# Attention probabilities enter the product with V undivided; the row sums are applied later, when the product is fetched for the merge

## The chip, the cores and the metric

One core of one Trainium2 chip runs the whole program. The metric is the device time of one execution in microseconds (us). PE is the engine for matrix products (TensorE), PEld its loading of weights, DVE VectorE, ACT ScalarE, POOL GpSimd, SP the engine that issues nearly all DMAs. Every engine works through its own instructions in order; they meet through semaphores.

## The reference, cut to what matters

One layer of an encoder for 1024 prompt tokens and 32 sample tokens. The part that matters here is sparse attention with 8 heads of 64 columns, and the merge behind it:

```
score  = indexer scores, masked block-causally;  idx = top-k keys per query
logits = (q . k_sel) / 8 + t5_bias ;  p = softmax(logits)          # per query row
a      = p . v_sel                                                   # (tokens, 512)
merged = sigmoid(g_A) * (a @ w_pa) + sigmoid(g_R) * (r @ w_pr)
x1     = LN(alpha * x + merged @ w_o);   y = LN(alpha * x1 + SwiGLU(x1))
```

`softmax` divides each row of exponentials by its sum. The division commutes with the product with V: it can be applied to a row of `p`, or to the same row of `a`.

## The kernel before, in words

All 1056 tokens are cut into nine tiles t (eight of 128, one of 32). Products are made in float32 by splitting each operand into a high and a low part (`split`: ACT writes `hi`, DVE or POOL the difference `lo`) and adding three products on PE.

PE's order is not left to the scheduler: a planner (`Weave`) keeps a clock `W.t` and one list of busy times for ACT, DVE and POOL ("a", "v", "p"), and every generator yields the planned time from which it may go on. The main generator issues a product, then every side generator whose time has come issues one. The order of the other engines is made by a scheduler from the program.

Around the change stand three pieces. `g_jobs` (main) makes the two branch gates: 16 blocks b of 24 column products for each of three column chunks j (384, 384, 288 tokens) into two PSUM banks `g`. While attention runs, ACT evicts them (L729); once attention is over (`"rt" in st`), DVE does (L726). `front` makes, for each head h and tile t, the bias plus mask on POOL (L774), the logits on PE (L783, L785), adds and takes the maximum on DVE (L787, with L795 where a row has two pieces, and L796), the exponential on ACT (L797), the reciprocal of the row sum (L799) and the scaled row (L800) on DVE, in place in `P`. `P_at` tells the planner when the row is ready. `back` transposes P on PE (L837, L838), splits it into `ph` and `pl`, multiplies by V (L861, L862; L867 for the sample tile), adds two halves (`av`, L878, L880) and stores the head's 64 columns to DRAM (`at_d`).

When the last head is done, `fetch` loads the retention output (`rT`) and the attention output (`aT`) of chunk 0 and `rT` of chunk 1, and splits them; the last gate chunks cover that. `aT` of chunks 1 and 2 is fetched when the gates are done, into memory that the activations x held until then. `c_jobs` then multiplies: for each block pair g, chunk j and block i, 24 products from `rT`, then 12 from `aT`, then the sigmoids, two products and a sum on DVE (L967, L968, L970), and a store.

Of the kernel before, what the change touches and what calls it, by code (L numbers as in the profile page):

```python
# [10 lines left out]
F32 = mybir.dt.float32  # L11
# [3 lines left out]
ALU = mybir.AluOpType  # L15
# [85 lines left out]
def mm(n, passes=1):  # L101
    return passes * max(256, n) / 2400.0


def body(ctx, tc, nc, a):
    W = Weave()
# [19 lines left out]
    def f32(ap):  # L126
        return ap.bitcast(F32)

    def dma(out, in_):
        nc.sync.dma_start(f32(out) if out.dtype == F32R else out, f32(in_) if in_.dtype == F32R else in_)  # L130
# [10 lines left out]
    ident = const.tile([128, 128], F32, name="ident")  # L141
    mhalf = const.tile([128, 4], F32, name="mhalf")

    def split(hi, lo, src, hi_eng="pool", lo_eng="pool"):
        if hi_eng == "pool":
            nc.gpsimd.tensor_scalar(hi, src, 1.0, 1.0, op0=ALU.mult, op1=ALU.mult)
        elif hi_eng == "act":
            nc.scalar.activation(hi, src, AF.Copy)  # L148
        else:
            nc.vector.tensor_copy(hi, src)  # L150
        e = nc.gpsimd if lo_eng == "pool" else nc.vector
        e.tensor_tensor(lo, src, f32(hi), op=ALU.subtract)  # L152
# [65 lines left out]
    def scratch(n, shape, name, dt=F32):  # L218
        return [dp.tile(shape, dt, name=f"{name}{i}") for i in range(n)]
# [5 lines left out]
    rt_d, at_d = scratch(1, [D, TT], "rtd")[0], scratch(1, [512, TT], "atd")[0]  # L225
    mt_d = [dp.tile([D, n], F32, name=f"mtd{j}") for j, (_, n) in enumerate(CHUNKS)]
    hd_d, x1_d = scratch(FB, [128, 1024], "hd"), scratch(1, [TT, D], "x1d")[0]
    r_d, r32_d = scratch(1, [8, 1152], "rd")[0], scratch(1, [8, 32, 1152], "r32")[0]

    xp = Open("xp")  # L230
# [16 lines left out]
    def mbank():  # L247
        return psum.tile([128, 512], F32, name="m", bufs=6)
# [261 lines left out]
    st = {}  # L510
# [221 lines left out]

    c_units = []

    def fetch(j, tl, dd, kt):
        c0, n = CHUNKS[j]
        hi, lo = tl
        for k in range(0, kt, 4):
            dma(lo[:, k:k + 4], dd[k * 128:(k + 4) * 128, c0:c0 + n].rearrange("(k p) c -> p k c", p=128))
            for z in range(k, k + 4, 2):  # L740
                split(hi[:, z:z + 2], lo[:, z:z + 2], f32(lo[:, z:z + 2]), "act", "dve")

    def to_attention():
        rp.close()
        xsp.close()
        tk.close()
        W.lag["v"] = 0.2
        st["att"] = True
        st["go"] = attention()

    def attention():
        ap = st["ap"] = Open("att", side="right")
# [4 lines left out]
            load_head(1, i)  # L757
        seq = [(h, t) for h in range(8) for t in range(9)]
        P, P_at, back_done, l_free = {}, {}, {}, []
        front_n = [0]  # L760
        NP = 6

        def front():
            for i, (h, t) in enumerate(seq):
                QS, KS, KL, TB, V = heads[h]
                c0, n = SEGS[t]
                Wd, k0, b0 = ((t + 1) * 128, 0, 896 - c0) if t < 8 else (LS, 1024, 896 - PAST)
                if i >= NP:
                    while seq[i - NP] not in back_done:
                        yield 0.0, W.t + 0.3  # L770
                    yield 0.0, back_done[seq[i - NP]]
                pp = ap.tile([128, 1024], F32, name="P", bufs=NP)
                P[h, t] = pp
                nc.gpsimd.tensor_tensor(pp[0:n, :Wd], TB[0:n, b0:b0 + Wd], masks[t][0:n, :], op=ALU.add)  # L774
                tt = W.on("p", 0.1 + Wd / 480, W.t)
                mx = ap.tile([128, 5], F32, name="mx", bufs=NP)
                halves = list(range(0, Wd, 512))
                for q, n0 in enumerate(halves):
                    nn = min(512, Wd - n0)
                    if len(l_free) >= 2:  # L780
                        yield 0.0, max(l_free[-2], tt - 1.0)
                    L = mbank()
                    nc.tensor.matmul(L[0:n, 0:nn], lhsT=QS[:, c0:c0 + n],  # L783
                                     rhs=KS[:, k0 + n0:k0 + n0 + nn], start=True, stop=False)
                    nc.tensor.matmul(L[0:n, 0:nn], lhsT=QS[:, c0:c0 + n],  # L785
                                     rhs=KL[:, k0 + n0:k0 + n0 + nn], start=False, stop=True)
                    nc.vector.tensor_tensor_reduce(out=pp[0:n, n0:n0 + nn], in0=L[0:n, 0:nn], in1=pp[0:n, n0:n0 + nn],  # L787
                                                   scale=1.0, scalar=-3e38, op0=ALU.add, op1=ALU.max,
                                                   accum_out=mx[0:n, q:q + 1])
                    c = 2 * mm(nn)  # L790
                    tt2 = W.on("v", 0.1 + nn / 930, max(tt, W.t + c))
                    l_free.append(tt2)
                    yield c, W.t
                if len(halves) == 2:
                    nc.vector.tensor_tensor(mx[0:n, 0:1], mx[0:n, 0:1], mx[0:n, 1:2], op=ALU.max)  # L795
                nc.vector.tensor_scalar(mx[0:n, 2:3], mx[0:n, 0:1], -1.0, None, op0=ALU.mult)  # L796
                nc.scalar.activation(pp[0:n, :Wd], pp[0:n, :Wd], AF.Exp, bias=mx[0:n, 2:3], scale=1.0,  # L797
                                     accum_out=mx[0:n, 3:4])
                nc.vector.reciprocal(mx[0:n, 4:5], mx[0:n, 3:4])  # L799
                nc.vector.tensor_scalar(pp[0:n, :Wd], pp[0:n, :Wd], mx[0:n, 4:5], None, op0=ALU.mult)  # L800
                tt = W.on("v", 0.2, tt2)
                tt = W.on("a", 0.35 + Wd / 1150, tt)
                P_at[h, t] = W.on("v", 0.2 + Wd / 1900, W.on("v", 0.1, tt))
                if t == 8 and h + 2 < 8:
                    for i in range(5):
                        load_head(h + 2, i)
                yield 0.0, W.t

        def back():
# [4 lines left out]
            while ia < len(items):  # L814
                opts = []
                if it < len(items) and it - ia < 3:
                    h, g, kb = items[it]
# [7 lines left out]
                h, g, kb = items[it if is_t else ia]  # L825
                last = 2 * g + 1 if g < 4 else 8
                c = 0 if kb < last else 128
                if is_t:
# [3 lines left out]
                    pt = mbank()  # L832
# [38 lines left out]
                if kb == last or g == 4:  # L871
                    for t in ((2 * g, last) if g < 4 else (8,)):
                        back_done[h, t] = W.t + cost
                    n, q0 = (256, g * 256) if g < 4 else (32, T)
                    u = ap.tile([64, 256], F32, name="av", bufs=2)
                    w = n if g < 4 else 64
                    nc.scalar.activation(u[:, :w], po[64:128, :w], AF.Copy)
                    nc.vector.tensor_tensor(u[:, :w], po[0:64, :w], u[:, :w], op=ALU.add)  # L878
                    if g == 4:
                        nc.vector.tensor_tensor(u[:, 0:32], u[:, 0:32], u[:, 32:64], op=ALU.add)  # L880
                    o_free = W.on("v", 0.35, W.on("a", 0.28, W.t + cost))
                    dma(at_d[h * 64:(h + 1) * 64, q0:q0 + n], u[:, :n])
                yield cost, W.t
            ap.close()
            st["hA"].close()
# [4 lines left out]
                  for j, (_, n) in enumerate(CHUNKS)]  # L890
            st["aT"] = [[st["rt"].tile([128, 4, n], F32R, name=f"aT{i}_{j}") for i in range(2)]
                        for j, (_, n) in enumerate(CHUNKS[:1])]
            st["rTt"] = rT
            fetch(0, rT[0], rt_d, 8)
            fetch(0, st["aT"][0], at_d, 4)
            fetch(1, rT[1], rt_d, 8)

        return front(), back()

    W.main(g_jobs())  # L900
# [22 lines left out]
    aT = st["aT"]  # L923
    for j, (_, n) in enumerate(CHUNKS):
        if j:
            aT.append([cp.tile([128, 4, n], F32R, name=f"aT{i}_{j}") for i in range(2)])
    fetch(1, aT[1], at_d, 4)
    fetch(2, rT[2], rt_d, 8)
    fetch(2, aT[2], at_d, 4)
    ringC = Open("ringC", bufs=3)  # L930

    def c_jobs():
# [77 lines left out]
    op = Open("wo", side="right")  # L1010
# [459 lines left out]
```

## Time and profile before

| | |
|---|---|
| runs, us | 1911.21, 1913.57, 1917.74; median 1913.57 |
| profiled execution, us | 1910.34, of which 1908.6 from the first to the last instruction |
| PE busy | 1860.3 us (97% of the span), 11361 products |
| DVE, ACT, POOL busy | 1308.2, 714.3, 741.8 us (69%, 37%, 39%) |
| mean granted PE clock | 0.993 of full |
| DMA | 233.12 MB, mean 122 GB/s |

Busy time is a mean over stages with different limits; where a stage can be shortened is read from the waits within it. A PE clock below 1 in a stretch means that products there took longer. Times in the rows below are from the start of the span.

### The profile page before, as it was taken

What the parts mean: (1) busy time and instruction counts of PE and PEld (TensorE: products, weight loads), DVE (VectorE), ACT (ScalarE), POOL (GpSimd) and SP (SyncE); (2) the same over time, 40 slices, a digit from 0 to 9 for tenths busy, and PEclk for the clock granted to TensorE, in tenths of its full rate; (3) what the DMA queues carried; (4) which work ended last, traced back from release to release, by engine and by line L of the source; (5) the groups of instructions that cost most, each with busy time, mean ns of one, the idle gap of its engine ahead of it and who ended that gap; (6) DMA issues with size and microseconds to landing.
All of it is one profiled execution on the core that took longest, in us unless ns stands there. A gap on an engine that the chain in (4) does not pass through costs nothing. (4 is left out here: it accounts for less than half of the span.)

```text
span 1908.6 us, 30961 instructions
## 1 busy us (share of the span) xinstructions
PE 1860.3 (97%) x11361; PEld 1687.5 (88%) x11361; DVE 1308.2 (69%) x2702; ACT 714.3 (37%) x1492; POOL 741.8 (39%) x741
## 2 busy tenths in 40 slices
PE   8999999999999999999999999999999999999998
PEld 7899899877888898899999879999999999877776
DVE  4799898999992877876533368855555555376667
ACT  5543422424333555555422246432333333432212
POOL 5345633455456435342321133143343333462211
PEclk9999999999999999999999999999999999999999
DMA  6245832223334765544644653122222222542212
GB/s 190 89 146 198 272 130 86 64 77 94 84 88 137 185 164 158 139 115 133 205 156 148 192 165 110 62 72 67 79 90 76 68 89 89 197 162 85 91 42 91
DMA packets 154368, 233.12 MB, mean 122 GB/s; under 512 B 18960, under 2 KB 118280, under 8 KB 154216
## 3 DMA queue, kind: packets, MB, share of 16 engines
q1 hardware_dynamic: 148168, 223.57, 37.6%
q10 hardware_dynamic: 6048, 7.57, 1.2%
q8 instruction: 89, 1.46, 0.3%
q14 instruction: 63, 0.52, 0.1%
HBM read 164.79 MB, written 67.48 MB: 122 GB/s over the span
## 5 line engine op out<-in xcount | busy, mean ns | idle before, releaser
L152 POOL TENSOR_TENSOR wlo<-raw,whi 128x1024 fp32r<-128x1024 f32 (+2 forms) x85 | 199.6, 2354 | 353.8 <-ACT whi L148 290.4
L148 ACT ACTIVATE whi<-raw 128x1024 fp32r<-128x1024 f32 (+1 forms) x158 | 137.1, 881 | 204.0 <-PE m L172 34.3
L172 PE MATMUL g<-xh,whi 128*128 128x384 f32 (+1 forms) x600 | 199.1, 332 | 5.7 <-DVE gev L726 5.7
L172 PE MATMUL g<-xh,wlo 128*128 128x384 f32 (+1 forms) x600 | 199.1, 332 | 0.2 <-POOL wlo L152 0.2
L172 PE MATMUL g<-xl,whi 128*128 128x384 f32 (+1 forms) x600 | 198.8, 331 | 0.0
L377 DVE MAX8 m<-sc 128x8 f32<-128x384 f32 (+6 forms) x209 | 182.4, 875 | 4.7
L378 DVE MATCH_REPLACE8 sc<-m,sc 128x384 f32<-128x384 f32 (+6 forms) x209 | 180.0, 861 | 0.2
L774 POOL TENSOR_TENSOR P<-TB,mask 128x128 f32<-128x128 f32 (+8 forms) x72 | 92.6, 1303 | 115.3 <-PE m L837 91.8
L172 PEld LDWEIGHTS g<-xh,whi 128*128 128x128 f32 x600 | 113.9, 190 | 8.8 <-DVE gev L726 6.2
L172 PEld LDWEIGHTS g<-xl,whi 128*128 128x128 f32 x600 | 114.0, 190 | 2.8 <-issue 1.1
L172 PEld LDWEIGHTS g<-xh,wlo 128*128 128x128 f32 x600 | 114.1, 190 | 2.4 <-POOL wlo L152 0.5
L1309 DVE TENSOR_TENSOR yo<-m,yo 128x512 f32<-128x512 f32 x128 | 85.4, 686 | 43.3 <-PE m L172 41.7
L1212 PE MATMUL m<-T,whi 128*128 128x264 f32 x624 | 114.6, 283 | 0.0
L172 PE MATMUL g<-whi,xl 128*128 128x512 f32 x256 | 105.4, 412 | 0.0
L172 PE MATMUL g<-whi,xh 128*128 128x512 f32 x256 | 104.9, 410 | 0.0
L172 PE MATMUL g<-wlo,xh 128*128 128x512 f32 x256 | 104.1, 407 | 0.0
L1212 PEld LDWEIGHTS m<-T,whi 128*128 128x128 f32 x624 | 96.6, 188 | 0.0
L172 PE MATMUL m<-rT,whi 128*128 128x384 f32 (+1 forms) x384 | 90.7, 322 | 0.0
L1192 POOL TENSOR_TENSOR raw<-raw,qs 128x512 f32<-128x512 f32 x20 | 32.0, 1602 | 149.5 <-DVE wlo L152 95.0
L1212 PE MATMUL m<-T,wlo 128*128 128x264 f32 x312 | 88.6, 284 | 0.0
L1212 PE MATMUL m<-x,whi 128*128 128x264 f32 x416 | 78.7, 288 | 4.4 <-DVE u L1220 4.1
L152 DVE TENSOR_TENSOR wlo<-raw,whi 128x512 fp32r<-128x512 f32 (+1 forms) x79 | 68.0, 874 | 18.3 <-ACT whi L148 17.4
(332 smaller groups left out, 5543.2 us busy)
## 6 DMA issues: line engine op xcount, KB each, us to landing
raw<-wT SPq DMA_DIRECT2D x33, 512.0 KB, 3.8
raw<-w_gate SPq DMA_DIRECT2D x22, 512.0 KB, 3.4
raw<-w_up SPq DMA_DIRECT2D x22, 512.0 KB, 3.4
hd<-sg SPq DMA_DIRECT2D x22, 512.0 KB, 3.2
raw<-w_down SPq DMA_DIRECT2D x22, 512.0 KB, 3.5
raw<-hd SPq DMA_DIRECT2D x22, 512.0 KB, 3.5
raw<-wr SPq DMA_DIRECT2D x16, 512.0 KB, 3.7
ml<-mtd SPq DMA_DIRECT2D x16, 512.0 KB, 4.6
```

Source lines behind the costliest of these rows:

```text
L148: nc.scalar.activation(hi, src, AF.Copy)
L152: e.tensor_tensor(lo, src, f32(hi), op=ALU.subtract)
L172: nc.tensor.matmul(out, lhsT=l, rhs=r, start=i == 0, stop=i == m - 1)
L377: nc.vector.max(m8[0:n], v)
L378: nc.vector.match_replace(v, m8[0:n], v, TAKEN)
L774: nc.gpsimd.tensor_tensor(pp[0:n, :Wd], TB[0:n, b0:b0 + Wd], masks[t][0:n, :], op=ALU.add)
L1192: nc.gpsimd.tensor_tensor(a12, a12, self.s2, op=ALU.subtract)
L1212: nc.tensor.matmul(o, lhsT=w[l][:, k, :], rhs=b[r][:, k, s], start=z < 4 and k == 0 and j == 0, stop=k == 3 and j == 2, skip_group_check=True)
L1309: nc.vector.tensor_tensor(y, src, y, op=ALU.add)
```

## The change

The exponential now writes its row sum into a tile `rsum` that holds the nine sums of a head in nine columns (set to 1.0 first, since the sample tile fills 32 rows only). The reciprocal and the scaling of P are gone, and the planner counts the row as ready when ACT is done with it. After the sample tile of a head, PE transposes `rsum` to nine rows of 128, DVE takes their reciprocal out of PSUM, and a DMA stores them to DRAM (`ri_d`). `fetch` of `aT` loads these rows again, each head's row spread over the 64 partitions of its columns (four DMAs for each half of a chunk, into one buffer `ri`), multiplies `aT` by them on DVE into `ri`, and splits from there.

```diff
+    ri_d = scratch(8, [9, 128], "ri")
...
-    def fetch(j, tl, dd, kt):
+    def fetch(j, tl, dd, kt, rows=False):
...
             for z in range(k, k + 4, 2):
-                split(hi[:, z:z + 2], lo[:, z:z + 2], f32(lo[:, z:z + 2]), "act", "dve")
+                src = f32(lo[:, z:z + 2])
+                if rows:
+                    ri = st["rt"].tile([128, 2, 384], F32, name="ri", bufs=1)
+                    for h in range(2 * z, 2 * z + 4):
+                        dma(ri[h % 2 * 64:h % 2 * 64 + 64, h // 2 - z, :].rearrange("p (t c) -> p t c", c=128),
+                            ri_d[h][None, c0 // 128:c0 // 128 + 3, :].to_broadcast([64, 3, 128]))
+                    nc.vector.tensor_tensor(ri[:, :, :n], src, ri[:, :, :n], op=ALU.mult)
+                    src = ri[:, :, :n]
+                split(hi[:, z:z + 2], lo[:, z:z + 2], src, "act", "dve")
...
+        rsum = {}
...
-                mx = ap.tile([128, 5], F32, name="mx", bufs=NP)
+                mx = ap.tile([128, 3], F32, name="mx", bufs=NP)
+                if t == 0:
+                    rsum[h] = ap.tile([128, 9], F32, name="rsum", bufs=2)
+                    nc.vector.memset(rsum[h], 1.0)
...
                 nc.scalar.activation(pp[0:n, :Wd], pp[0:n, :Wd], AF.Exp, bias=mx[0:n, 2:3], scale=1.0,
-                                     accum_out=mx[0:n, 3:4])
-                nc.vector.reciprocal(mx[0:n, 4:5], mx[0:n, 3:4])
-                nc.vector.tensor_scalar(pp[0:n, :Wd], pp[0:n, :Wd], mx[0:n, 4:5], None, op0=ALU.mult)
+                                     accum_out=rsum[h][0:n, t:t + 1])
                 tt = W.on("v", 0.2, tt2)
-                tt = W.on("a", 0.35 + Wd / 1150, tt)
-                P_at[h, t] = W.on("v", 0.2 + Wd / 1900, W.on("v", 0.1, tt))
+                P_at[h, t] = W.on("a", 0.35 + Wd / 1150, tt)
...
                     dma(at_d[h * 64:(h + 1) * 64, q0:q0 + n], u[:, :n])
+                    if g == 4:
+                        pt = mbank()
+                        nc.tensor.transpose(pt[0:9, 0:128], rsum[h], ident)
+                        rr = ap.tile([9, 128], F32, name="rrow", bufs=1)
+                        nc.vector.reciprocal(rr, pt[0:9, 0:128])
+                        dma(ri_d[h], rr)
...
-            fetch(0, st["aT"][0], at_d, 4)
+            fetch(0, st["aT"][0], at_d, 4, True)
...
-    fetch(1, aT[1], at_d, 4)
+    fetch(1, aT[1], at_d, 4, True)
     fetch(2, rT[2], rt_d, 8)
-    fetch(2, aT[2], at_d, 4)
+    fetch(2, aT[2], at_d, 4, True)
```

The change also moves instructions, in three places. Outside attention, the transition behind it and the merge, the order on every engine is as before (two of the memsets stand ahead of attention).

First, PE within a head. The planner fills PE's planned waits in attention with gate products. From the first logits to the last product with V it now places 475 gate products where it placed 843; the other 368 follow behind attention, so that 22 gate chunks are evicted by DVE there instead of 6. Here is the stretch of PE at the start of the fourth head, from the products with V to the transposes of its tiles 4 and 5 (`P`; `m` is a PSUM bank, `g` a gate bank). Before:

```order
L838 MATMUL m<-ident,P 128x128
L861 MATMUL m<-ph,V 128x256
L862 MATMUL m<-pl,V 128x256
L861 MATMUL m<-ph,V 128x256
L862 MATMUL m<-pl,V 128x256
L172 MATMUL g<-xh,wlo 128x384
L172 MATMUL g<-xh,whi 128x384
L172 MATMUL g<-xl,whi 128x384
...
L837 MATMUL m<-ident,P 128x128
L838 MATMUL m<-ident,P 128x128
```

The line of dots stands for four more gate products. And now:

```order
L848 MATMUL m<-ident,P 128x128
L871 MATMUL m<-ph,V 128x256
L872 MATMUL m<-pl,V 128x256
L871 MATMUL m<-ph,V 128x256
L872 MATMUL m<-pl,V 128x256
L847 MATMUL m<-ident,P 128x128
L848 MATMUL m<-ident,P 128x128
```

The seven gate products ahead of the transposes are gone. From the logits of tile 3 of this head to these transposes PE has 16 gate products where it had 27.

Second, DVE at the same place: from the logits of tile 3 to those of tile 5. Before:

```order
L796 TENSOR_SCALAR mx<-mx 128x1
L878 TENSOR_TENSOR av<-m,av 64x64
L880 TENSOR_TENSOR av<-av 64x32
L787 ISA P,mx<-m,P 128x512
...
L787 ISA P,mx<-m,P 128x128
L787 ISA mx 128x1
L799 RECIPROCAL mx<-mx 128x1
L795 TENSOR_TENSOR mx<-mx 128x1
L800 TENSOR_SCALAR P<-P,mx 128x512
L796 TENSOR_SCALAR mx<-mx 128x1
```

And now (L800 is here the former L787, L808 the former L795, L809 the former L796):

```order
L897 RECIPROCAL rrow<-m 9x128
L789 MEMSET rsum 128x9
L809 TENSOR_SCALAR mx<-mx 128x1
L888 TENSOR_TENSOR av<-m,av 64x64
L800 ISA P,mx<-m,P 128x512
...
L800 ISA P,mx<-m,P 128x128
L800 ISA mx 128x1
L890 TENSOR_TENSOR av<-av 64x32
L808 TENSOR_TENSOR mx<-mx 128x1
L809 TENSOR_SCALAR mx<-mx 128x1
```

The scaling of tile 3 and its reciprocal no longer stand ahead of the maximum of tile 4 (the last row of both pieces); a reciprocal of nine rows and a memset stand ahead of the maximum of tile 3 (the first row of the piece before, the third of the piece now).

Third, the merge: what SP issues once its chunks begin. `aT` of chunks 1 and 2 and the first gate rows stand where they stood; the rows `ri` come in groups of four between them (numbers are those of the DRAM tiles, one for each head):

```order
L130 DMA raw<-w_pa 128x1024
L130 DMA raw<-w_pr 128x1024
L130 DMA ri<-ri_140 64x384
L130 DMA ri<-ri_141 64x384
L130 DMA ri<-ri_142 64x384
L130 DMA ri<-ri_143 64x384
L130 DMA mtd_110<-mm 128x384
L130 DMA ga<-ga_91 128x384
L130 DMA gr<-gr_99 128x384
L130 DMA raw<-w_pr 128x1024
L130 DMA mtd_110<-mm 128x384
L130 DMA ga<-ga_92 128x384
```

Before, the first two of these rows were followed at once by the store of `mm`. Two more such groups follow, for the two halves of chunk 2; the group for the first half of chunk 1 is issued while the gates still run.

## Rows read from the trace of the kernel before

**Rows 1.** Stretches: length; busy PE, PEld, DVE, ACT, POOL; PE clock, DMA share, GB/s.

```profile
613.80:886.50 272.70, 261.75 (x1762) 249.22 (x1761) 210.52 (x701) 152.90 (x406) 119.82 (x82) 0.99 0.54 145
886.50:919.00 32.50, 26.83 (x156) 26.19 (x155) 18.06 (x23) 13.33 (x19) 4.75 (x2) 0.95 0.65 226
919.00:949.00 30.00, 30.00 (x184) 30.00 (x183) 12.57 (x19) 14.29 (x22) 10.56 (x5) 1.00 0.65 220
```

**Rows 2.** Timeline of PE in attention: products that PE waited for (idle before).

```profile
627.36 0.58 PE L862 MATMUL m<-pl,V 128*128 128x256 f32 x1 [2.31 <-DVE pl L152]
664.66 0.33 PE L838 MATMUL m<-ident,P 128*128 128x128 f32 x1 [1.66 <-DVE mx L796]
...
696.68 0.33 PE L838 MATMUL m<-ident,P 128*128 128x128 f32 x1 [0.28 <-DVE mx L796]
...
731.24 0.33 PE L838 MATMUL m<-ident,P 128*128 128x128 f32 x1 [2.47 <-DVE mx L796]
...
798.28 0.47 PE L838 MATMUL m<-ident,P 128*128 128x128 f32 x1 [2.54 <-DVE P L800]
```

**Rows 3.** Timelines of DVE, ACT and POOL ahead of the wait that ends at 731.24.

```profile
725.57 1.45 DVE L880 TENSOR_TENSOR av<-av 64x32 f32<-64x32 f32 x1
...
727.87 0.97 DVE L795 TENSOR_TENSOR mx<-mx 128x1 f32<-128x1 f32 x1
728.76 2.42 DVE L800 TENSOR_SCALAR P<-P,mx 128x512 f32<-128x512 f32 x1
...
725.97 0.18 ACT L797 ACTIVATION_READ_ACCUMULATOR P<-P,mx 128x1 f32 x1
...
725.31 5.59 POOL L774 TENSOR_TENSOR P<-TB,mask 128x768 f32<-128x768 f32 x3
```

**Rows 4.** Timeline of DVE one head earlier: the scaling of tiles 3 and 5.

```profile
696.15 0.47 DVE L800 TENSOR_SCALAR P<-P,mx 128x512 f32<-128x512 f32 x1
...
701.22 0.62 DVE L800 TENSOR_SCALAR P<-P,mx 128x768 f32<-128x768 f32 x1
```

**Rows 5.** Lines L800, L799 and L795 (min/median/max ns, first and last start).

```profile
L800 DVE TENSOR_SCALAR P<-P,mx x72: 286/549/2640, 620.5 to 877.4; 128x128 f32<-128x128 f32 x8, 128x256 f32<-128x256 f32 x8, 128x384 f32<-128x384 f32 x8, 128x512 f32<-128x512 f32 x8
...
L799 DVE RECIPROCAL mx<-mx x72: 140/153/167, 619.9 to 877.2; 128x1 f32<-128x1 f32 x64, 32x1 f32<-32x1 f32 x8
...
L795 DVE TENSOR_TENSOR mx<-mx x40: 136/159/1860, 627.7 to 875.8; 128x1 f32<-128x1 f32 x32, 32x1 f32<-32x1 f32 x8
```

**Rows 6.** Timeline of PE: two gate products, one behind the other.

```profile
732.02 0.34 PE L172 MATMUL g<-xh,wlo 128*128 128x384 f32 x1
732.20 0.34 PE L172 MATMUL g<-xh,whi 128*128 128x384 f32 x1
```

**Rows 7.** The stretch behind the wait that ends at 798.28 (columns as in rows 1).

```profile
798.30:810.00 11.70, 11.70 (x65) 11.35 (x66) 9.36 (x33) 6.76 (x16) 2.03 (x2) 0.88 0.44 130
```

**Rows 8.** Transition: the longest wait of PE, and the splits of rT on DVE (grouped by line).

```profile
909.83 0.45 PE L172 MATMUL g<-xh,whi 128*128 128x384 f32 x1 [4.72 <-DVE gev L726]
...
L152 DVE TENSOR_TENSOR rT<-rT,rT 128x768 fp32r<-128x768 f32 (+1 forms) x12 | 11.6, 1017 | 6.9 <-ACT rT L148 6.9
```

**Rows 9.** DMAs: issue of a row block on SP, and landing (KB each, median us).

```profile
L130 SPq DMA_DIRECT2D atd<-av x40: 445/452/467, 631.5 to 890.8; - x40
...
atd<-av SPq DMA_DIRECT2D x32, 64.0 KB, 1.9
...
ga<-ga SPq DMA_DIRECT2D x4, 192.0 KB, 4.0
```

**Rows 10.** Timelines of ACT, DVE and POOL in the merge.

```profile
924.95 2.85 ACT L148 ACTIVATE aT<-aT 128x768 fp32r<-128x768 f32 x4 [3.86 <-DMA aT<-atd]
...
932.25 2.48 DVE L970 TENSOR_TENSOR mm<-ga,gr 128x384 f32<-128x384 f32 x1
...
938.41 0.56 DVE L970 TENSOR_TENSOR mm<-ga,gr 128x384 f32<-128x384 f32 x1
...
931.90 5.09 POOL L152 TENSOR_TENSOR wlo<-raw,whi 128x1024 fp32r<-128x1024 f32 x2 [6.92 <-ACT whi L148]
```

## The prediction

> **What bounds the kernel now.** The page first: PE is busy for 97% of the span, so work taken off DVE is worth only what PE waits for it. How much that is, the stretches around the change say [rows 1]. In the first, attention (613.8 to 886.5), PE is busy for 261.75 of 272.70 us: 10.95 us idle. In the transition (886.5 to 919.0) it is 5.67 idle. In the first chunks of the merge it is none. The reader is to see that DVE is at 77% in attention and still not the bound: its busy time counts only at the moments when PE stands still.
>
> Next, where those moments are [rows 2]. One wait of 2.31 us belongs to the start. The others come once in each head, at the transposes of tiles 2 and 3, and are of two sizes: three of 1.66, 2.47 and 2.54 us, and four of 0.27 to 0.30, of which one stands in the rows. Two more, of 0.16 and 0.60, lie elsewhere. Sum: 10.9.
>
> Then the large ones taken apart [rows 3]. ACT had finished the exponential at 726.15. The row was usable only at 731.18, since DVE came to its scaling late and the scaling itself took 2.42 us, where the same shape one head earlier took 0.47 [rows 4]. POOL was working through three additions from 725.31 to 730.90; the all-SBUF steps of DVE (0.97 us for one column, then 2.42) end about when POOL's instructions do. Over the run the scaling lasts from 0.29 to 2.64 us, its median 0.55 [rows 5].
>
> This is what a rule of the Trainium skill states (SBUF — State Buffer, "Who interferes with whom"): VectorE and GpSimd share one pair of SBUF ports, and an instruction of VectorE that uses both ports, or reads two SBUF operands, waits for the whole of GpSimd's instruction. The trace agrees here: 2.42 against 0.47 us.
>
> **The change part by part.** *Scaling and reciprocal removed.* In a head without the block, from the logits of tile 3 to the finished rows of tiles 4 and 5, DVE loses three reciprocals of 0.153 [rows 5], one scaling of 0.47, one of 0.62, and one of the width between, which I take at 0.54 as an estimate from these two [rows 4]: 2.1 us. It gains a reciprocal of nine rows and a memset, which the trace does not show; each lies between nothing and the 0.47 of the scaling, and nearest to the one-column reciprocal, so 0.15 to 0.2 each. The chain gets about 1.75 us shorter. PE's cover over the same stretch loses 11 gate products, which follow one another at 0.18 us [rows 6]: 2.0 us shorter, less the transpose added. The planner has taken as much cover away as the chain gave back. So heads that waited 0.3 us will wait about that again, 0.3 to 0.6. What really goes is the blocked scaling, in three heads. The one-column maximum L795 (up to 1.86 us [rows 5]) and L880 stay and can still be blocked, so I take 0.5 us for each of seven heads: 3.5, plus the 2.31 of the start and the 0.76 elsewhere, 6.6 in place of 10.95. **Term: -4.4.** Bounds: all head waits gone, -7.8; each head waiting for an L795 blocked at its longest, 7 x 1.86 + 3.1 = 16.1, +5.1.
>
> *Clock.* After the 2.54 us wait the granted clock is 0.88 over 11.7 us [rows 7], 1.4 us lost; most of that goes with the wait. **Term: -1.2** (0 to -1.4).
>
> *Transposes of the sums.* Eight, on PE, and their results are waited for by no product. Each has a third of the columns of a gate product that takes 0.18; the row of a transpose that was waited for shows 0.33 for its whole length [rows 2]. I take 0.11 each: **+0.9** (0.5 to 2.6).
>
> *Gate products moved.* 368 of them leave attention, where they took the same 0.18 us, and form a run without anything between. They cost the same there; evictions move from ACT to DVE, which then has little else. **0.** If PE had to wait for an eviction it would be in the transition, next.
>
> *Transition.* Today PE waits 4.72 us there, for an eviction that stands on DVE behind splits of `rT` and `aT` [rows 8]. With the change the fourth gate eviction again stands behind eight DVE instructions of that kind: four of `rT`, one multiplication, one of `aT`, two of `rT` (before: six of `rT`, two of `aT`). The rows `ri` put 0.39 MB into a transfer queue that is busy, 1.7 us at the 226 GB/s of the stretch [rows 1]. The multiplication makes a chain of three (DVE, ACT, DVE), but `rT` arrives no earlier than that ends. **0**, between -1.5 and +2.5.
>
> *Merge.* This is where the change adds a wait. Counted from the first merge product (919.0, the third stretch), PE comes to the second half of `aT` of chunk 1 at 17.9 us (two chunks of 6.3, then 24 + 6 products at 0.18), and to the second half of chunk 2 at 29.2. `aT` lands at 5.95 [rows 10], and the split follows at once today, so PE has 10 us to spare. Now the single buffer `ri` makes the four halves serial: multiply (1.0, as a split of `rT` [rows 8]), ACT 0.8 [rows 10], DVE 0.9, then four issues of 0.45 us [rows 9], then the landing of 98 KB. For the landing the trace gives 1.9 us for 64 KB in attention and 4.0 for 192 KB in this very stretch [rows 9]; I take 2.7. First half split at 8.8, new rows at 13.3. There two of POOL's subtractions run, from 12.9 to 18.0 [rows 10], and an all-SBUF sum of DVE took 2.48 us next to them against 0.56 without [rows 10]. So the multiplication ends near 16.4, ACT at 17.2, DVE near 19: PE is 1 to 1.5 us late. Two more rounds of 2.1 to 2.7 for the work and 4.5 for the rows bring the last half to about 33 against the 29.2 of the plan. All waits of the merge together are that lateness, between 2 and 4: **+3.0**. Bounds: nothing, if POOL is not in the way and the rows land in 1.9 us (the last half is then ready at 27.3); 7, if they land in 4.0 and each multiplication is blocked.
>
> By the port rule above the multiplication, which reads two SBUF operands, must wait for POOL's instruction. By it the merge costs about 3; if it did not hold for this operation, close to nothing. This changes only how near the lower bound is.
>
> **Sum:** -4.4 - 1.2 + 0.9 + 0 + 0 + 3.0 = -1.7 us, against the profiled execution of 1910.34: 1908.6. The median of the runs stands 3.2 us above that execution, so 1911.9; I say **1912**. That is no change that a measurement of this kernel can tell (about 0.3%, 5.7 us, on either side of 1913.6: below 1907.8 or above 1919.3).
>
> **The rivals.**
> *Full gain.* All head waits vanish (-7.8), and the rows come in time (merge 0): -7.8 - 1.2 + 0.9 = -8.1, so 1905.5. For it: in the unblocked heads the exponential ends well before PE needs the row. Against: the cover of 11 gate products has gone too.
> *The row loads are slow.* One mechanism, in the merge: each group of `ri` takes long to land since it stands behind weights of 512 KB. PE is late by 1 us for each us of landing, in two of the three groups. At 5.3 us the merge costs 3.0 + 5.2, and with a drop of the clock after such a wait (1.4, rows 7) the whole is +4.9, 1918.5; from 5.7 us on the kernel is slower than 1919.3. For it: 4.0 us for the `ga` rows in this stretch. Against: 1.9 for blocks of nearly this size in attention.
>
> A page of the skill (DMA: Bandwidth & Descriptors, "Issuing engines are not separate DMA queues") has every transfer share the same 16 engines. [...]
>
> *New waits in the heads.* With 475 gate products in place of 843, ACT has its 152.90 us of work [rows 1], a little less for 16 evictions that move to DVE, in about 212 us: some 70% where it was 56%. If PE comes to wait for it, or for a blocked L795, by 1.3 us in each head, attention keeps its 10.95 or so: 9.1 + 3.1 - 10.95 = +1.2, the clock term stays away, and the sum is +1.2 + 0.9 + 3.0 = +5.1: 1918.7. It decides for slower from 1.4 us per head.
>
> **How the numbers follow.** Forecast 0.45 (1907 to 1916 by itself), full gain 0.20, slow rows 0.17, new waits 0.18. Faster by over 0.3%: nearly all of the full gain and a fifth of the forecast, 0.27. Slower: somewhat under half of the two late rivals, 0.16. The same: 0.57. The range reaches down past the full gain, since waits elsewhere may go with it, and up to the point where the two late rivals have begun to count as slower: 1903 to 1921.
>
> **What would show it.** In the profile after: no L799 and no L800 of that kind; attention about 60 us shorter (368 products at 0.18 us, a third of them narrower) and the run of gates behind it as much longer; in attention, waits of PE for the exponential or the maximum of 0.3 to 1 us per head, none near 2.5. In the transition one wait of 4 to 7 us for a gate eviction. In the merge, waits of PE at the first `aT` products of chunks 1 and 2 for DVE's split, 2 to 4 us together, and in front of them DMA `ri` landing in 2 to 4 us. The prediction is wrong if the merge shows no wait, if the heads still wait over 1 us each, or if the clock falls in a stretch where it is full now.

## The result, and the profile after

The changed kernel takes 1925.01 us (median of six, 1922.13 to 1929.01), the kernel before 1912.39 in runs beside it: 1.0068 times as long, 95% interval 1.0056 to 1.0079. It is slower by 12.6 us, where 1912 had been forecast. The execution profiled is the longest, 1929.01 us with a span of 1927.2.

Four stretches of the changed kernel, by the columns of [rows 1]: attention, from the first logits to the last product with V; the gate products behind it; the merge up to the end of its longest wait; and 6.3 us behind that wait.

```profile
620.70:840.40 219.70, 207.83 (x1397) 190.93 (x1395) 165.57 (x571) 138.83 (x386) 102.59 (x74) 0.98 0.59 152
840.40:929.40 89.00, 84.71 (x509) 84.39 (x510) 25.31 (x40) 17.95 (x22) 16.99 (x7) 0.96 0.48 156
929.40:963.80 34.40, 29.43 (x176) 28.86 (x174) 16.14 (x20) 12.55 (x20) 10.27 (x4) 0.98 0.67 226
964.70:971.00 6.30, 6.30 (x32) 6.30 (x33) 1.56 (x4) 0.94 (x4) 2.38 (x1) 0.63 0.37 101
```

Attention is 52 us shorter than before (271.55 us between the same two products), and PE is idle in it for 11.87 us: somewhat longer than before (10.95), although DVE has 45 us less to do there. The waits have changed places. The timeline of PE, products that it waited for (line numbers are those of the changed kernel, where L800 is the sum with the bias and no longer the scaling):

```profile
630.28 0.38 PE L871 MATMUL m<-ph,V 128*128 128x256 f32 x1 [1.35 <-ACT ph L148]
636.81 0.39 PE L872 MATMUL m<-pl,V 128*128 128x256 f32 x1 [0.70 <-DVE pl L152]
...
683.84 0.50 PE L796 MATMUL m<-KS,QS 128*128 128x512 f32 x1 [1.67 <-DVE mx L809]
713.39 0.80 PE L796 MATMUL m<-KS,QS 128*128 128x512 f32 x1 [2.15 <-DVE mx L800]
743.71 0.33 PE L848 MATMUL m<-ident,P 128*128 128x128 f32 x1 [0.68 <-ACT P L810]
...
820.22 0.50 PE L796 MATMUL m<-KS,QS 128*128 128x512 f32 x1 [1.84 <-DVE av L888]
```

Before, the large ones within the heads stood at the transposes of tiles 2 and 3 and were the scaling of P [rows 2]. Now three of 1.67 to 2.15 us stand at logits (L796), which need a bank that DVE has yet to empty, and four of 0.60 to 0.70 at the transposes of tiles 4 and 5, for the exponential (L810). What DVE did ahead of the wait that ends at 713.39, and POOL beside it:

```profile
708.58 1.63 DVE L890 TENSOR_TENSOR av<-av 64x32 f32<-64x32 f32 x1
710.13 2.36 DVE L808 TENSOR_TENSOR mx<-mx 128x1 f32<-128x1 f32 x1
712.52 0.15 DVE L809 TENSOR_SCALAR mx<-mx 128x1 f32<-128x1 f32 x1
712.64 0.69 DVE L800 CUSTOM_DVE_ANT_0 P<-m,P 128x512 f32<-128x512 f32 x1
```

```profile
706.15 4.00 POOL L784 TENSOR_TENSOR P<-TB,mask 128x896 f32<-128x896 f32 x2
710.12 2.35 POOL L152 TENSOR_TENSOR wlo<-raw,whi 128x1024 fp32r<-128x1024 f32 x1
```

The maximum of one column, L808, takes 2.36 us and ends with POOL's subtraction (712.49 and 712.47). It is the former L795 [rows 5]. Five of its 40 executions last over 0.9 us, and each ends within 0.03 us of an instruction of POOL. The sum ahead of it, L890, ends with POOL's addition in the same way (710.21 and 710.15). That POOL holds these steps up is read from such ends; no run moved POOL's work.

The merge, 140.7 us before from its first product to its last sum, is 149.0. PE's waits in it, then the issues of SP and the steps of DVE and ACT that lead to the longer one:

```profile
948.16 0.45 PE L172 MATMUL m<-aT,whi 128*128 128x384 f32 x1 [0.71 <-DVE aT L152]
963.87 0.61 PE L172 MATMUL m<-aT,whi 128*128 128x288 f32 x1 [4.34 <-ACT aT L148]
```

```profile
948.16 2.37 SPq L130 DMA_DIRECT2D ri<-ri  x4
950.57 0.58 SPq L130 DMA_DIRECT2D gr<-gr  x1
...
957.68 2.37 SPq L130 DMA_DIRECT2D ri<-ri  x4
```

```profile
953.15 0.76 DVE L748 TENSOR_TENSOR ri<-aT,ri 128x576 f32<-128x576 f32 x1 [3.25 <-DMA ri<-ri]
...
956.89 0.76 DVE L152 TENSOR_TENSOR aT<-ri,aT 128x576 fp32r<-128x576 f32 x1 [2.51 <-ACT aT L148]
...
962.35 0.76 DVE L748 TENSOR_TENSOR ri<-aT,ri 128x576 f32<-128x576 f32 x1 [3.17 <-DMA ri<-ri]
```

```profile
955.76 0.53 ACT L982 ACTIVATE gr<-gr 128x384 f32<-128x384 f32 x1 [4.97 <-DMA gr<-gr]
956.19 0.67 ACT L148 ACTIVATE aT<-ri 128x576 fp32r<-128x576 f32 x1
...
963.14 0.68 ACT L148 ACTIVATE aT<-ri 128x576 fp32r<-128x576 f32 x1 [4.38 <-DVE ri L748]
```

To be read from below: the last half (963.14) waits for its multiplication, that for rows issued at 957.68, and these for the buffer, which the half before left with its split at 957.65. That half had been multiplied by 953.91, but stood on ACT behind a sigmoid, whose gate row SP had issued only behind four `ri` loads (950.57). And after the wait of 4.34 us PE's granted clock is 0.63 over 6.3 us (0.98 in the stretch that holds the merge up to it); in the first 4.3 of these it is 0.50, the lower of its two levels, 1.2 GHz.

### The profile page after: what moved, and what is told of

Read it like the earlier page. It is cut to its first block, busy times and chain, and to the rows that moved or that the text cites. A ratio compares the mean times of both kernels' runs of the same rounds, so it can differ in the third digit from the quotient of the medians.

```text
span 1927.2 us, 30975 instructions
## 1 busy us (share of the span) xinstructions
PE 1874.2 (97%) x11369; PEld 1697.6 (88%) x11369; DVE 1273.8 (66%) x2596; ACT 704.2 (37%) x1476; POOL 741.1 (38%) x741
## 3 DMA queue, kind: packets, MB, share of 16 engines
q10 hardware_dynamic: 3744, 4.72, 0.8%
```

## The experiments

One table for all. "Waits" are the idle times of PE of over 0.1 us, summed; they and the stages are of one profiled execution each, the medians of four to twelve executions. The stages are bounded by the first logits product, the first product from `rT` and the last sum of the merge. The ratio is that to the kernel before, whose medians in runs beside these lay between 1910.9 and 1912.4.

| | median, us | ratio, 95% interval | attention and gates, us | waits in attention | waits in the gates behind | merge, us | waits in it |
|---|---|---|---|---|---|---|---|
| before | 1912.4 | 1 | 301.9 | 10.88 | 5.67 | 140.7 | 0 |
| changed | 1925.0 | 1.0068 (1.0056-1.0079) | 308.7 | 11.12 | 4.29 | 149.0 | 5.24 |
| e1 old order | 1916.2 | 1.0028 (1.0016-1.0039) | 294.6 | 5.06 | 6.50 | 153.4 | 8.58 |
| e2 separate buffers | 1916.5 | 1.0031 (1.0018-1.0044) | 306.9 | 11.06 | 4.40 | 142.2 | 1.26 |
| e3 both | 1908.1 | 0.9977 (0.9966-0.9989) | 297.1 | 5.05 | 9.10 | 142.5 | 1.59 |
| e5 no rows applied | 1911.8 | 1.0004 (0.9994-1.0014) | 305.7 | 11.47 | 3.36 | 140.7 | 0 |
| e6 before, new order | 1939.1 | 1.0138 (1.0122-1.0153) | 334.4 | 35.06 | 3.36 | 140.7 | 0 |
| e7 e2, rows later | 1912.4 | 1.0004 (0.9994-1.0015) | 300.1 | 8.68 | 4.97 | 142.6 | 1.63 |
| e8 e2, DVE charged | 1906.4 | 0.9966 (0.9954-0.9978) | 292.4 | 4.17 | 4.46 | 142.5 | 1.56 |
| e9 e3, fused maximum | 1901.1 | 0.9941 (0.9927-0.9955) | 286.6 | 0 | 6.67 | 145.2 | 2.69 |
| e10 e9, rows early | 1900.9 | 0.9945 (0.9928-0.9962) | 290.7 | 0 | 10.45 | 143.0 | 2.08 |
| e11 e2, fused maximum | 1901.7 | 0.9951 (0.9939-0.9963) | 292.0 | 1.59 | 4.22 | 144.5 | 2.05 |
| e12 before, fused maximum | 1905.1 | 0.9968 (0.9954-0.9981) | 294.1 | 6.51 | 5.33 | 140.7 | 0 |
| e13 e9, more banks | 1898.6 | 0.9922 (0.9905-0.9940) | 277.6 | 0 | 0 | 151.7 | 7.95 |

**The two losses.** The theory was that PE's denser order costs the time in attention, and the chain through the single buffer `ri` that in the merge. The first edit gives the planner its old costs back:

```diff
-                P_at[h, t] = W.on("a", 0.35 + Wd / 1150, tt)
+                tt = W.on("a", 0.35 + Wd / 1150, tt)
+                P_at[h, t] = W.on("v", 0.2 + Wd / 1900, W.on("v", 0.1, tt))
```

> The changed kernel, but the planner counts a row of P as ready as late as before the change, so that PE's order within attention is the old one (843 gate products between the first logits and the last product with V) with the eight transposes added; the merge is unchanged. Theory A (the denser order of PE costs the time in attention): attention and gates together, 301.9 us before and 308.7 after the change, come to 298 to 301, the merge stays near 149, the kernel takes 1914 to 1918, 7 to 11 us less than the changed one. Rival B (the added work itself costs it: transposes, the memset, the reciprocal of nine rows, the waits for them): attention and gates stay at 306 to 309, the kernel at 1922 to 1926.

8.8 us less than the changed kernel. Attention and gates take even less than expected, 294.6 us, and the merge of this execution more, 153.4, with waits of 8.58: the chain of rows is still in it.

The second gives the rows of chunks 1 and 2 two buffers each, in the pool of the merge:

```diff
-                    ri = st["rt"].tile([128, 2, 384], F32, name="ri", bufs=1)
+                    ri = rows.tile([128, 2, 384], F32, name=f"ri{j}", bufs=nb)
...
-    fetch(1, aT[1], at_d, 4, True)
+    fetch(1, aT[1], at_d, 4, cp, 2)
```

> The changed kernel, but the rows of chunks 1 and 2 have a buffer for each half of a chunk, so that none waits for the split of the one before; all else as changed. Theory A (the chain through the single buffer costs the time in the merge: 8.3 us, of which 5.2 are waits of PE and the rest products at the lower clock behind them): the merge goes from 149.0 to 141 to 143 us, the kernel to 1917 to 1919. Rival B (the 16 issues on SP and the multiplications beside POOL cost it, whatever the buffers): PE still waits 3 us or more for the attention chunks or, now, for the gate rows issued behind the 16; merge 146 or more, kernel 1922 or more.

8.5 us less; the merge takes 142.2 us, with one wait of 1.26. The chain through the buffer was most of the loss in the merge, 6.8 of 8.3 us. Both edits together:

> Both edits together: the old planner's costs and a buffer for each half. If the two losses are independent and both theories A hold: attention and gates 298 to 301, merge 141 to 143, the kernel 1907 to 1911, below the kernel before (1912.4) by 1 to 5 us. If only the planner's order counts: 1914 to 1918; if only the buffers: 1917 to 1919; if neither: 1922 to 1926.

16.9 us less than the changed kernel (8.8 + 8.5 = 17.3): the losses add up, and this version is faster than the kernel before. All of PE's waits in attention and the gates that the timeline shows:

```profile
661.57 0.51 PE L796 MATMUL m<-KS,QS 128*128 128x512 f32 x1 [0.63 <-DVE mx L809]
726.75 0.50 PE L796 MATMUL m<-KS,QS 128*128 128x512 f32 x1 [1.55 <-DVE mx L809]
792.12 0.50 PE L796 MATMUL m<-KS,QS 128*128 128x512 f32 x1 [2.01 <-DVE mx L800]
838.11 0.38 PE L872 MATMUL m<-ph,V 128*128 128x256 f32 x1 [0.85 <-ACT ph L148]
904.41 0.69 PE L172 MATMUL g<-xh,whi 128*128 128x384 f32 x1 [9.10 <-DVE gev L727]
```

The waits at the transposes are gone, with the scaling. Those at the logits of three heads remain. The last prices the rows as a whole (`fetch` with `rows=False` everywhere):

> The changed kernel without the rows in the fetch: the attention output is split as it was before the change, so the division by the sums is left out (the sums are still transposed, inverted and stored). Prices the whole of loading and applying the rows, in the transition and the merge. If the rows are the merge's loss: merge 140.7 as before, the kernel 1925 - 8.3 = 1916 to 1918, with attention and gates near 308. If the merge's loss was a stroke of the clock in one run: 1922 or more.

13.2 us less than the changed kernel and level with the kernel before. So all of the loss hangs on the rows, and attention as changed is worth nothing, neither gain nor loss. Of the 13.2, the single buffer is 8.5. Between the two profiled executions the merge differs by 8.3 us and the gates behind attention by 2.0; where the rest lies these runs do not show.

**What the order costs, and which of the planner's costs makes it.** The order by itself: the kernel before, still dividing P, in the new order.

> The kernel before with one edit: the planner no longer counts the reciprocal and the scaling of P, which are still done. PE's order in attention is then the changed kernel's (475 gate products where there were 843). Theory A (the order by itself costs the time, whatever DVE does): attention and gates, 301.9 us before, come to 312 to 325, since the scaling that takes up to 2.6 us now also lies in the shorter gaps; the kernel at 1922 to 1936. Rival B (the order is harmless and the new small operations of the change cost the time): attention and gates 300 to 304, the kernel 1911 to 1915.

27.6 us more than before, beyond the range of theory A: 28 of the 35 us of waits are at transposes, in nearly every head, for example

```profile
692.94 0.48 PE L837 MATMUL m<-ident,P 128*128 128x128 f32 x1 [2.97 <-DVE mx L796]
...
724.16 0.48 PE L837 MATMUL m<-ident,P 128*128 128x128 f32 x1 [2.90 <-DVE P L800]
```

Removing the division from this order (e5) brings 27.3 us; the order that the removal made the planner choose had cost 27.6. That is where the expected gain went. Once the division is gone, the same order still costs 8.4 us (e2 against e3). Which of the two effects of the old cost spread the order, the charge on DVE's list or the later time of the row?

> The changed kernel with the separate row buffers, and the planner counting a row of P as ready 0.3 us + width/1900 later, without charging DVE for it. The planner places 502 gate products in attention (475 without the edit). Theory A (what spread PE's order was the charge on DVE's list, which paces the logits, and not the time at which a row counts as ready): near the kernel with the buffers alone, 1913 to 1917. Rival B (the time of the rows is what counts, since PE waits at their transposes): the gain of the old costs comes back, 1907 to 1910.

> The changed kernel with the separate row buffers, and the planner charging DVE for the reciprocal and the scaling that are no longer done, but counting the row as ready when ACT is done. The planner places 836 gate products in attention. Theory A (the charge spreads the order): 1907 to 1910, as with the old costs (1908.1). Rival B (the time of the rows counts): 1913 to 1917.

The charge alone brings 10.1 us and 836 gate products back; it spreads the order. The later time, with 502 products, brings 4.1, more than theory A allowed and less than B. It counts as well, and the two are not cleanly told apart; both together (e3) gain no more than the charge alone.

**The step that remains: the maximum of one column.** It is done with the change of sign in one instruction, whose second tile is a scalar for each partition:

```diff
                 if len(halves) == 2:
-                    nc.vector.tensor_tensor(mx[0:n, 0:1], mx[0:n, 0:1], mx[0:n, 1:2], op=ALU.max)
-                nc.vector.tensor_scalar(mx[0:n, 2:3], mx[0:n, 0:1], -1.0, None, op0=ALU.mult)
+                    nc.vector.tensor_scalar(mx[0:n, 2:3], mx[0:n, 0:1], mx[0:n, 1:2], -1.0, op0=ALU.max, op1=ALU.mult)
+                else: nc.vector.tensor_scalar(mx[0:n, 2:3], mx[0:n, 0:1], -1.0, None, op0=ALU.mult)
```

> The version with the old costs and the separate buffers, and the maximum of the two pieces of a row (two tiles of one column) done in one instruction with the sign change, as a tensor_scalar with a scalar from a tile. Theory A (the waits of 0.6 to 2.0 us that are left at the logits of three heads, 4.2 us together, are that one-column maximum, held up beside POOL: 2.14 and 2.36 us in the trace where it takes 0.16 alone): the fused operation stays at 0.15 to 0.3, the waits go, 1903 to 1905 against 1908.1. Rival B (the fused operation is held up as well, or the wait is the bank's): no change, 1907 to 1909.

7.0 us less than e3, and PE has no wait of over 0.1 us in attention. The line as it was in the changed kernel (min/median/max ns), then in this version, where 15 of its 40 executions start while an instruction of POOL runs:

```profile
L808 DVE TENSOR_TENSOR mx<-mx x40: 139/149/2356, 626.6 to 828.5; 128x1 f32<-128x1 f32 x32, 32x1 f32<-32x1 f32 x8
```

```profile
L808 DVE TENSOR_SCALAR mx<-mx x40: 192/202/215, 627.6 to 862.7; 128x1 f32<-128x1 f32 x32, 32x1 f32<-32x1 f32 x8
```

The same in the dense order, then in the kernel before:

> The changed kernel's dense order (475 gate products in attention), with the separate buffers and the fused maximum. Theory A (the dense order exposes every short chain from product to eviction to product): only the waits at the logits go (5.7 of 11.1 us), those at the transposes and the products with V stay; 1909 to 1913. Rival B (the dense order costs only because the held-up maximum has no cover): attention without waits, 1901 to 1905, as the version with the old costs and the fused maximum (1901.1).

> The kernel before, with one edit: the fused maximum. Theory A (the waits of the kernel before at the transposes, 7.8 of 10.9 us, are mostly the scaling of P held up beside POOL, so removing the division is what pays): waits of 7 to 10 us remain in attention, 1908 to 1912. Rival B (the held-up maximum ahead of it is as much to blame, so that the same gain is to be had without the change): waits fall to 5 us or less, 1904 to 1907.

In the dense order it brings 14.8 us (1916.5 to 1901.7), and theory A falls: with the held-up maximum gone the dense order costs nothing that can be told from the old one (1901.1; the two intervals overlap, though e11's profiled execution, its longest, has attention and gates 5.4 us longer). What waits remain are small and in the first head, as this one:

```profile
625.80 0.39 PE L872 MATMUL m<-pl,V 128*128 128x256 f32 x1 [0.56 <-DVE pl L152]
```

So the dense order does not cost by itself; it lays bare the maximum that POOL holds up. Not every held-up step counts: the sum L890 takes up to 1.94 us in e11 still, and no wait comes of it. In the kernel before the time is rival B's too: 5.8 us come from the maximum alone. The waits in attention, 6.51, lie between the two forecasts; none for the scaling is over 1 us, though it is held up as before:

```profile
L800 DVE TENSOR_SCALAR P<-P,mx x72: 285/686/2169, 625.1 to 875.4; 128x128 f32<-128x128 f32 x8, 128x256 f32<-128x256 f32 x8, 128x384 f32<-128x384 f32 x8, 128x512 f32<-128x512 f32 x8
```

Against this run e9, with the division moved, is 4.0 us shorter; the two intervals just touch, so that this gain is barely clear of the noise.

**The transition.** PE still waits there for one eviction, 6.67 us in e9. On DVE the eviction (L727) stands behind the multiplication of chunk 0, which waits for its rows:

```profile
891.84 1.55 DVE L748 TENSOR_TENSOR ri<-aT,ri 128x768 f32<-128x768 f32 x1 [1.57 <-DMA ri<-ri]
894.30 0.96 DVE L152 TENSOR_TENSOR aT<-ri,aT 128x768 fp32r<-128x768 f32 x1 [0.91 <-ACT aT L148]
895.18 1.82 DVE L152 TENSOR_TENSOR rT<-rT,rT 128x768 fp32r<-128x768 f32 x2
896.91 0.45 DVE L727 COPY gev<-g 128x288 f32<-128x288 f32 x1
```

Two edits on that: the eight loads for chunk 0 go to buffers of their own and are issued by ACT ahead of the loads of `rT` (`nc.scalar.dma_start`); and the last gate products go to other banks.

> The version with the old costs, the separate buffers and the fused maximum, and the rows of chunk 0 in buffers of their own, issued by ACT (which stands idle there) as soon as the last head is done, not by SP behind the loads of the retention output. Theory A (PE's 6.67 us in the transition is an eviction that stands on DVE behind the multiplication, and that behind its late rows): the multiplication waits for no rows, PE's wait goes to 3.5 to 5 us, 1897 to 1900 against 1901.1. Rival B (the transition is bound by the loads of the retention output, at some 380 GB/s): the wait stays at 6 to 7.5 us, 1900 to 1903.

```diff
-                o = gbank()
+                o = mbank() if "rt" in st else gbank()
```

> The version with the old costs, the separate buffers and the fused maximum, and the last gate chunks (behind attention) accumulated in the six banks that stand empty there, not in the two gate banks. Theory A (PE's 6.67 us in the transition are a bank that waits for DVE, whose queue waits for loads; the lower clock behind it is its sequel): no wait there, the merge starts 8 to 10 us earlier and still finds its chunks, 1891 to 1896. Rival B (the loads bind the transition: the wait only moves to the first attention products of the merge, which need rows and chunks that land no earlier): the merge waits 4 us or more, 1898 to 1903.

In both runs the time is rival B's. In e10 the multiplication waits 0.17 us, but `rT` comes later in its place, and PE's wait grows to 10.45 in the profiled execution; the time is that of e9. In e13 the wait in the gates is gone and stands 12 us later, at the attention products of the merge that take the second half of chunk 0:

```profile
909.22 0.69 PE L172 MATMUL m<-aT,whi 128*128 128x384 f32 x1 [7.64 <-ACT aT L148]
```

What SP and DVE did ahead of it:

```profile
894.75 0.96 DVE L152 TENSOR_TENSOR aT<-ri,aT 128x768 fp32r<-128x768 f32 x1 [0.91 <-ACT aT L148]
...
902.37 2.90 DVE L152 TENSOR_TENSOR rT<-rT,rT 128x576 fp32r<-128x576 f32 x2 [0.87 <-ACT rT L148]
905.20 3.09 DVE L748 TENSOR_TENSOR ri<-aT,ri 128x768 f32<-128x768 f32 x1
```

```profile
895.74 2.37 SPq L130 DMA_DIRECT2D ri<-ri  x4
```

The rows of this half are issued when the split of the first half leaves the buffer (895.71), which chunk 0 has singly in e13 as in e9; and the multiplication takes 3.09 us beside a subtraction of POOL (904.58 to 907.47), where the first half's took 0.96. e13 has the lowest time of all, 1898.6, but its interval meets that of e9. Whether the loads that come due when attention ends bind this place, or the buffer of chunk 0 and the steps that POOL holds up on DVE, these two runs do not decide: e10 gave chunk 0 its two buffers but kept the gate banks, and the two edits were not run together.

## Why the prediction missed

The sum was -1.7 us; measured were +12.6. By e5 the miss of 14.3 falls into 10.2 for the rows (13.2 against +3.0 for the merge and 0 for the transition) and 4.3 for the rest (-0.4, that is 1911.8 against 1912.2, where -4.4 - 1.2 + 0.9 = -4.7 stood); the two add up to 14.5, since the kernel before is compared in two sets of runs. **Two steps failed.** The larger is the size of the merge term, whose mechanism was right; in the smaller, attention, the places of the waits were wrong as well.

**Merge, +3.0: the place and the mechanism were right, the size was not** (8.3 in the profiled executions, 13.2 for the rows as a whole in the medians). The chain came out closely up to its middle: first half split 8.8 us after the first merge product (8.8 measured), rows landing in 2.7 us (2.8), PE late by 0.71 at the second half of chunk 1 (1 to 1.5). Two things were missing. An issue takes 0.59 us here, not 0.45, and behind four of them stood a gate row, and behind that row's sigmoid on ACT the next half: what else stands ahead of a step was looked for on DVE, not on SP and ACT. The last half was ready after 35.2 us, not 33. And the clock fell after the wait: of the 8.3 us 5.24 are waits, and most of the rest are products at 1.2 GHz. That sequel stood in a rival and not in the term.

**Attention, -4.4: the step that failed** is the one that gave seven heads 0.5 us each. It began rightly: the planner takes about as much cover away as the chain gives back, and L795 "can still be blocked". But that was priced as an exception. The waits came to 11.12 us where 6.6 stood, within the bounds (+5.1), and e11 shows the cause: in e2 they are 11.06, and without the held-up maximum 1.59. The places were wrong as well. I looked at the transposes, where the waits were, and not at the logits, which wait for a bank that the held-up DVE has not emptied.

**Clock, -1.2**: nothing was gained. The granted clock of attention is 0.98 after 0.99, and waits elsewhere brought stretches at 1.2 GHz of their own, as behind the one of 4.34 us.

**Transposes, +0.9**: not tested alone; -0.4 holds it. The reciprocal of nine rows takes 0.95 us, where 0.15 to 0.2 was taken from the one-column reciprocal; the memset 0.07.

**Gate products moved, 0**: right within the noise of the medians, as e11 against e9 shows.

**Transition, 0**: about right for PE's wait, one of 4.29 us for an eviction where there were two, of 0.95 and 4.72 [rows 8]. Without the rows (e5) it is 3.36. The rows of chunk 0 are eight loads, 0.79 MB, not the 0.39 that was reckoned with.

**The rivals.** New waits in the heads came true, L808 being its second named cause, but not to the point that decides for slower. In the seven later heads the waits at logits and transposes sum to 8.25 us, 1.18 each on average, where it had 1.3, and 1.4 for slower; PE's idle time stays near its 10.95, as this rival said. Slow rows had the right place and the wrong cause: the buffer, not the landing. The groups of 96 KB landed in 2.8 us in the merge; the 1.9 and 4.0 between which it was weighed are of 64 and 192 KB. New waits and a dearer merge came together, which no case of mine held, and that lies outside the range that was built from one at a time.

## What to carry to other kernels

When a planner is told that a step is gone, it spends the time at once, as cover that it no longer plans; what the kernel gains is then decided by the steps that the planner's costs do not know. Look for these first, by the largest against the median time of each small operation (2356 and 149 ns here), and then test whether PE waits for them: mending this one took two lines and brought 5.8 us without the change and 7.0 or 14.8 with it, where the change with its two losses mended (e3) brought 4.1. And give data that is loaded late a buffer for each use, since a single one chains its load to the last step of the use before, through every queue on the way.

## What was not expected of the hardware

A one-column operation on two tiles can last until POOL's instruction beside it ends, up to 2.36 us, where the same work with one of the tiles as a scalar for each partition stays within 192 to 215 ns in 40 executions, 15 of them started beside a running instruction of POOL. This holds for one column: the scaling of P, wide rows with a scalar for each partition, takes up to 2169 ns in e12, against a median of 686. A reciprocal of 9 x 128 values from a bank takes 946 ns, one of 128 x 1 in the kernel before 153 (median, [rows 5]); whether the difference lies in the values of a row or in the bank was not tried apart. A load that spreads one row over 64 partitions takes 0.59 us to issue, a store of a block of rows 0.45 [rows 9].
